# The experts' last 32 slots on 512-wide column tiles with half of the contraction each, in front of the wide products of their stages

## The chip, the cores and the metric

The kernel runs on one core of a Trainium2 chip. The metric is the device time of one execution in microseconds (us); less is better. Engines are called as in the profile: TensorE (PE; its weight loads are PEld), VectorE (DVE), ScalarE (ACT), GpSimd (POOL) and SyncE (SP), which here issues most of the DMAs.

## The reference, cut to what matters

One decoder layer: a mixer of gated linear attention and dilated attention, then a hierarchical mixture of experts, each with a residual, and a final norm. 2048 tokens of 1024 features, 32 experts with 512 hidden features, two experts for a token. The change is in the experts alone:

```python
def expert_block(args):
    toks, e = args
    xb = x[toks]
    hb = jax.nn.silu(xb @ w1[e]) * (xb @ w3[e])
    return hb @ w2[e]
...
y = y.reshape(R, D).astype(jnp.float32) * row_w[:, None]
out = jnp.zeros((M, D), jnp.float32).at[row_tok].add(y)
```

All data are float32. `x` is 2048 x 1024, `w1[e]` and `w3[e]` are 1024 x 512, `w2[e]` is 512 x 1024.

## The kernel before

The part that matters is `moe`. A table in memory holds for each expert 160 slots of a token and its gate. The first 128 slots of an expert are its wide part, the last 32 its narrow part; tokens beyond these go to a loop at the end that is not touched here apart from the call of `up`, `across` and `down`.

Weights. `weights` (L1272) loads the weights of an expert as six tiles `raw` of 128 x 2048 floats, 1 MB each, in the order w1a, w3a, w1b, w3b, w2a, w2b, where a and b are the halves of the contraction. The loads are issued on SyncE's queue; the pool has six buffers. L1288 splits each tile: ScalarE casts it to `hi`, VectorE subtracts and gives `lo`; pool of five buffers each.

Wide part. `turn` (L1310) transposes the 128 gathered tokens (eight transposes on TensorE into `tp`) and splits them into `nh` and `nl`. `up` (L1327) makes 48 products of 128 x 512 for an expert, three for each eighth of the contraction and each of w1 and w3 (L1338 to L1340), in the order w1a, w3a, w1b, w3b, into two PSUM tiles. L1352 and L1353 make `h` of them (silu on ScalarE, product on VectorE). `across` (L1362) transposes `h` (L1365) and splits it into `hh` and `hl` (L1368). `down` (L1378) makes 24 products (L1387 to L1389), scales them by the gate into `y` and adds `y` to the rows of `acc` in memory with an indirect DMA on GpSimd (L1394).

Narrow part. `turn_last` (L1319) transposes the last slots of four experts at once, `R`, into `nr`, which is not split. TensorE multiplies them with the raw float32 weights. A product of only 32 slots fills 32 of 128 columns of the array, so four products stand beside each other in four column groups (`tile_position=(0, 32 * g)`), each with its own 32 partitions of the result `pr`. In `up` the four groups are two halves of 256 columns of w1 and two of w3, each over the full contraction: 8 x 4 matmuls of 256 columns (L1347), behind the 48 wide products in the program. A float32 matmul is two records in the profile, so these are 64. L1358 and L1359 make `hr`, L1373 transposes it, L1375 copies it to `ht`. In `down` the groups are four quarters of w2's 1024 columns: 4 x 4 matmuls of 256 columns (L1402), 32 records, behind the 24 wide products and behind the issue of L1394. L1405 scales the 128 x 256 result into `yr`, and L1406 adds its 128 rows of 1 KB to `acc4`, `acc` seen as quarter rows, at the rows `i4`, which L1203 to L1205 make of the slot table `ir`.

Order. The loop over the experts (L1416) writes for each one: the loads and splits, the gather for the expert after the next, `up`, `across`, `turn` of the next expert, at every fourth expert `turn_last` of the next four, then `down`. This order is only a priority: a scheduler takes, engine by engine and by its own estimate of durations, the first instruction in program order that is ready, and what it finds is the fixed order of that engine's queue. Each engine then works through its queue in order and waits for semaphores where needed. `self.behind` gives single pairs an order. After expert 1, `order` sorts the tokens so that those that are through early can be finished (`finish`: gather of `acc`, norm, scatter to the output) while the last experts run.

Of the kernel before, what the change touches and what calls it, by code (L numbers as in the profile page):

```python
# [56 lines left out]
class Layer:  # L57
# [1113 lines left out]
    def moe(self):  # L1171
        tc, nc, a = self.tc, self.nc, self.a
        with self.moest as st:
# [9 lines left out]
            acc4 = self.acc.rearrange("t (g c) -> (t g) c", g=4)  # L1183
# [3 lines left out]
            i4A = keep.tile([128, NE], I32, name="i4")  # L1187
# [3 lines left out]
            def entries(es):  # L1191
# [10 lines left out]
                f4 = gp.tile([128, NE], F32, name="f4", bufs=1)  # L1202
                nc.vector.tensor_copy(f4[:, es], irA[:, es, 0])  # L1203
                nc.vector.tensor_scalar(f4[:, es], f4[:, es], 4.0, self.gcol, OP.mult, OP.add)
                nc.vector.tensor_copy(i4A[:, es], f4[:, es])  # L1205
# [121 lines left out]
            def up(w, x, nr=None):  # L1327
# [26 lines left out]
                hr = None  # L1354
                if nr is not None:
                    hr = gp.tile([128, 256], F32, name="hr")
                    by, to = (lambda t: t.rearrange("t (p k) -> t k p", k=2)), hr[64:128].rearrange("t (k p) -> t k p", k=2)
                    nc.scalar.activation(to, by(pr[0:64]), AF.Silu)  # L1358
                    nc.vector.tensor_tensor(to, by(pr[64:128]), to, OP.mult)  # L1359
                return h, hr  # L1360

            def across(h, hr):  # L1362
# [3 lines left out]
                hh = gp.tile([128, 4, 128], F32R, name="hh")  # L1366
                hl = gp.tile([128, 4, 128], F32R, name="hl")
                self.crossed = nc.scalar.copy(hh, tp), nc.vector.tensor_tensor(hl, tp, hh.bitcast(F32), OP.subtract)  # L1368
                ht = None
                if hr is not None:  # L1370
                    tr = rps.tile([128, 2, 64], F32, name="r")
                    for c in range(2):
                        nc.tensor.transpose(tr[:, c, :], hr[64:128, c * 128:(c + 1) * 128], self.ident[64:128, 64:128])  # L1373
                    ht = gp.tile([128, 2, 2, 32], F32, name="ht")
                    nc.vector.tensor_copy(ht, tr.rearrange("p c (u s) -> p u c s", u=2))  # L1375
                return hh, hl, ht

            def down(w2, x, it, irs, e=None):  # L1378
                hh, hl, ht = x
# [16 lines left out]
                if ht is not None:  # L1396
                    ir, i4 = irs
                    pr = rps.tile([128, 256], F32, name="r")
                    for k in range(4):
                        raw = w2[k // 2][0]  # L1400
                        for g in range(4):
# [151 lines left out]
```

## Time and profile before

| | us |
|---|---|
| median of 3 runs | 2216.52 |
| lowest, highest | 2212.23, 2219.35 |
| profiled execution | 2223.29 |
| its span | 2221.3 |

Busy times in the span: TensorE 2086.3 us (94%), weight loads 1567.7 (71%), VectorE 1272.1 (57%), ScalarE 1060.2 (48%), GpSimd 474.5 (21%). DMA queues moved 436.59 MB. The experts begin at about 1310 us, with a first expert that waits for its data, and from about 1600 us they run evenly up to 2155 us; after that come the last wide products and the end of the norm.

How to read it: a timeline row has the start and length of an instruction (of several of one kind in a row the count, and the length from the first start to the last end), its engine, line, operation, what it writes and reads, and in brackets how long its engine was idle before it and for whom it waited. The length of a matmul contains its way through the array, so lengths overlap, and what one costs is read from the step to the start of the next. A row of a list of lines gives for all instructions of one line and shape the count, the busy time and the mean length in ns, and behind the second bar the idle time of the engine before them. The clock is the share of 2.4 GHz that TensorE was granted.

### The profile page before, as it was taken

The page shows a single profiled execution, that of the slowest core. Times are in us where ns is not written, and L with a number is a line of the kernel's source. Part 1 is how long each engine was busy: PE and PEld are TensorE (multiplying, and loading weights), DVE is VectorE, ACT ScalarE, POOL GpSimd, SP SyncE. Part 2 cuts the span into 40 slices and gives each one's busy share as a digit, 9 for nine tenths or more (in the row PEclk, how much of TensorE's full clock was granted, in tenths as well). Part 3 has the DMA queues.
Part 4 walks back from the last instruction along what each step waited for, and adds up shares of the span by engine and source line. Part 5 has one row for each costly group of instructions (what it writes and reads, how often), then busy time and mean ns, then how long its engine had stood idle before and what let it go on. Part 6 is the DMA issues. An engine that isn't in the chain of part 4 may idle for free. (4 is left out here: it accounts for less than half of the span.)

```text
span 2221.3 us, 38624 instructions
## 1 busy us (share of the span) xinstructions
PE 2086.3 (94%) x15306; PEld 1567.7 (71%) x15306; DVE 1272.1 (57%) x2452; ACT 1060.2 (48%) x1809; POOL 474.5 (21%) x362
## 2 busy tenths in 40 slices
PE   7999999999997999999999968899999999999990
PEld 7799889799885766666667756567676766767760
DVE  5203336424435466666656766567767677777663
ACT  5412335523323366867723334355555555555552
POOL 2000000000002012351321342523212222222235
PEclk9999999999998999999999969999999999999995
DMA  8333333333316524453368728688888888878886
GB/s 254 109 124 100 114 124 110 102 113 124 109 68 190 178 68 138 146 135 100 88 204 279 238 80 293 198 290 305 298 294 281 307 308 304 305 279 287 307 277 234
DMA packets 189033, 436.59 MB, mean 197 GB/s; under 512 B 35041, under 2 KB 106530, under 8 KB 162978
## 3 DMA queue, kind: packets, MB, share of 16 engines
q1 hardware_dynamic: 139090, 347.65, 44.5%
q0 software_dynamic: 21488, 60.36, 10.4%
q10 hardware_dynamic: 28272, 26.09, 4.0%
q8 instruction: 122, 2.00, 0.4%
q14 instruction: 61, 0.50, 0.1%
HBM read 342.48 MB, written 92.08 MB: 196 GB/s over the span
## 5 line engine op out<-in xcount | busy, mean ns | idle before, releaser
L1288 DVE TENSOR_TENSOR lo<-raw,hi 128x2048 fp32r<-128x2048 f32 x192 | 438.8, 2289 | 121.8 <-ACT hi L1288 121.4
L1288 ACT CAST hi<-raw 128x2048 fp32r<-128x2048 f32 x192 | 365.1, 1906 | 198.5 <-DMA raw<-expert_w 181.0
L564 ACT ACTIVATE P<-P,st 128x256 f32<-128x256 f32 (+1 forms) x384 | 173.9, 455 | 96.8 <-DVE st L562 92.5
L213 PE MATMUL mm<-whi,nh 128*128 128x256 f32 x768 | 219.9, 286 | 0.0
L215 PE MATMUL mm<-whi,nl 128*128 128x256 f32 x768 | 218.1, 284 | 0.0
L214 PE MATMUL mm<-wlo,nh 128*128 128x256 f32 x768 | 217.7, 284 | 0.0
L1340 PE MATMUL mm<-lo,nh 128*128 128x512 f32 x512 | 207.3, 406 | 0.1
L1338 PE MATMUL mm<-hi,nh 128*128 128x512 f32 x512 | 204.6, 400 | 1.1 <-ACT nh L1316 1.1
L1339 PE MATMUL mm<-hi,nl 128*128 128x512 f32 x512 | 201.4, 393 | 0.0
L128 POOL TENSOR_TENSOR ss<-ss,mhalf 128x1 f32<-128x1 f32 (+3 forms) x40 | 34.6, 865 | 699.1 <-DVE ss L127 698.9
L562 DVE CUSTOM_DVE_ANT_0 P<-s,amask 128x256 f32<-128x256 f32 (+1 forms) x384 | 124.9, 362 | 66.2 <-PE s L558 42.6
L190 PE MATMUL mm<-nh,whi 128*128 128x512 f32 x384 | 154.5, 402 | 0.0
L191 PE MATMUL mm<-nl,whi 128*128 128x512 f32 x384 | 153.1, 399 | 0.0
L192 PE MATMUL mm<-nh,wlo 128*128 128x512 f32 x384 | 152.7, 398 | 0.0
L213 PEld LDWEIGHTS mm<-whi,nh 128*128 128x128 f32 x768 | 145.4, 189 | 2.0 <-issue 0.7
L214 PEld LDWEIGHTS mm<-wlo,nh 128*128 128x128 f32 x768 | 145.7, 190 | 0.8 <-DVE wlo L176 0.4
L215 PEld LDWEIGHTS mm<-whi,nl 128*128 128x128 f32 x768 | 144.9, 189 | 0.1
L1347 PE MATMUL r<-raw,nr 128*32 128x256 f32 x2048 | 143.0, 383 | 0.0
L1394 POOL DMA_INDIRECT acc<-y,it x32 | 93.9, 2934 | 228.7 <-ACT y L1391 222.5
L558 PE MATMUL s<-k,q 64*128 64x256 f32 (+1 forms) x768 | 132.8, 416 | 0.3 <-DVE st L562 0.3
L1340 PEld LDWEIGHTS mm<-lo,nh 128*128 128x128 f32 x512 | 96.7, 189 | 43.1 <-issue 19.4
L176 DVE TENSOR_TENSOR wlo<-raw,whi 128x1024 fp32r<-128x1024 f32 x48 | 57.0, 1221 | 112.7 <-ACT whi L175 112.7
(340 smaller groups left out, 4165.0 us busy)
## 6 DMA issues: line engine op xcount, KB each, us to landing
raw<-expert_w SPq DMA_DIRECT2D x192, 1024.0 KB
raw<-w_in ACTq DMA_DIRECT2D x48, 512.0 KB
fb<-fac SPq DMA_DIRECT2D x24, 384.0 KB
x<-x SPq DMA_DIRECT2D x16, 512.0 KB
og<-og SPq DMA_DIRECT2D x32, 256.0 KB
xr<-x SPq DMA_DIRECT2D x32, 256.0 KB
v<-av SPq DMA_DIRECT2D x8, 1024.0 KB
hp<-xr SPq DMA_DIRECT2D x32, 256.0 KB
```

Of the source, the lines that this page charges most:

```text
L190: nc.tensor.matmul(ps, hi[:, k, ms], nh[q][:, k, :], start=k == 0, stop=False)
L191: nc.tensor.matmul(ps, hi[:, k, ms], nl[q][:, k, :], start=False, stop=False)
L192: nc.tensor.matmul(ps, lo[:, k, ms], nh[q][:, k, :], start=False, stop=k == KD - 1)
L213: nc.tensor.matmul(ps[:, j, :], h, hi[:, k, :], start=j == 0 and k == 0, stop=False, skip_group_check=True)
L214: nc.tensor.matmul(ps[:, j, :], h, lo[:, k, :], start=False, stop=False, skip_group_check=True)
L215: nc.tensor.matmul(ps[:, j, :], l, hi[:, k, :], start=False, stop=k == KD - 1, skip_group_check=True)
L564: nc.scalar.activation(P[:, h, 0:w], P[:, h, 0:w], AF.Exp, bias=nm, scale=-1.0, accum_out=dn)
L1288: split = nc.scalar.copy(hi, raw), nc.vector.tensor_tensor(lo, raw, hi.bitcast(F32), OP.subtract)
L1338: nc.tensor.matmul(ps[m], nh[:, k, :], hi[:, kk, :], start=k == 0, stop=False)
L1339: nc.tensor.matmul(ps[m], nl[:, k, :], hi[:, kk, :], start=False, stop=False)
L1340: nc.tensor.matmul(ps[m], nh[:, k, :], lo[:, kk, :], start=False, stop=k == KD - 1)
L1347: nc.tensor.matmul(pr[32 * g:32 * g + 32], nr[:, k, :], raw[:, k % 4, (g % 2) * 256:(g % 2) * 256 + 256], start=k == 0, stop=k == KD - 1, ...
```

## The change

The narrow part gets functions of its own. `up_last` has 16 matmuls of 512 columns instead of 32 of 256: the four column groups are now w1 and w3 with their full 512 columns, each for an even and an odd eighth of the contraction. The two partial sums lie in different partitions of `pr`, so ScalarE copies one pair to `sm`, VectorE adds the other, and then silu and product follow, on 32 partitions of 512 columns. `down_last` has 8 matmuls of 512 columns instead of 16 of 256, with two halves of w2's columns times two eighths of the contraction; the two parts are scaled and added by ScalarE and VectorE, and `yr` has 64 rows of 2 KB, added at the rows `i2` of `acc2` (half rows). `up_last` stands in front of `up` in the program, `down_last`, with the transposes of `hr` and the addition of `yr`, in front of `down`. The tiles `h`, `hh`, `hl`, `hr` and `ht` have one buffer instead of two.

```diff
-                f4 = gp.tile([128, NE], F32, name="f4", bufs=1)
-                nc.vector.tensor_copy(f4[:, es], irA[:, es, 0])
...
+                f2 = gp.tile([64, NE], F32, name="f2", bufs=1)
+                nc.vector.tensor_copy(f2[:, es], irA[0:64, es, 0])
...
+            def up_last(w, nr):
+                pr = rps.tile([128, 512], F32, name="r")
+                for k in range(0, KD, 2):
+                    for g in range(4):
+                        kk, raw = k + g // 2, w[g % 2][k // 4][0]
+                        nc.tensor.matmul(pr[32 * g:32 * g + 32], nr[:, kk, :], raw[:, kk % 4, :],
+                                         start=k == 0, stop=k == KD - 2, skip_group_check=True, tile_position=(0, 32 * g))
+                hr = gp.tile([128, 256], F32, name="hr", bufs=1)
+                sm = gp.tile([64, 512], F32, name="sm", bufs=1)
+                sg = gp.tile([64, 512], F32, name="sg", bufs=1)
+                nc.scalar.copy(sm, pr[64:128])
+                nc.vector.tensor_tensor(sm, pr[0:64], sm, OP.add)
+                nc.scalar.activation(sg[32:64], sm[0:32], AF.Silu)
+                by = lambda t, u: t[:, 256 * u:256 * u + 256].rearrange("t (p k) -> t k p", k=2)
+                for u in range(2):
+                    to = hr[64 + 32 * u:96 + 32 * u].rearrange("t (k p) -> t k p", k=2)
+                    nc.vector.tensor_tensor(to, by(sm[32:64], u), by(sg[32:64], u), OP.mult)
+                return hr
...
-                pr = None
-                if nr is not None:
-                    pr = rps.tile([128, 256], F32, name="r")
-                    for k in range(KD):
-                        for g in range(4):
-                            raw = w[g // 2][k // 4][0]
-                            nc.tensor.matmul(pr[32 * g:32 * g + 32], nr[:, k, :], raw[:, k % 4, (g % 2) * 256:(g % 2) * 256 + 256],
-                                             start=k == 0, stop=k == KD - 1, skip_group_check=True, tile_position=(0, 32 * g))
-                h = gp.tile([128, 512], F32, name="h")
+                h = gp.tile([128, 512], F32, name="h", bufs=1)
...
+            def down_last(w2, hr, ir, i2, e):
+                ht = across_last(hr)
+                pr = rps.tile([128, 512], F32, name="r")
+                for k in range(0, 4, 2):
+                    raw = w2[k // 2][0]
+                    for g in range(4):
+                        kk, f = g // 2, g % 2
+                        nc.tensor.matmul(pr[32 * g:32 * g + 32], ht[:, k // 2, kk, :], raw[:, kk, f * 512:f * 512 + 512],
+                                         start=k == 0, stop=k == 2, skip_group_check=True, tile_position=(0, 32 * g))
+                yr = yp.tile([64, 512], F32, name="yr", bufs=2)
+                nc.scalar.activation(yr, pr[64:128], AF.Copy, scale=ir[64:128, 1:2].bitcast(F32))
+                nc.vector.scalar_tensor_tensor(yr, pr[0:64], ir[0:64, 1:2].bitcast(F32), yr, op0=OP.mult, op1=OP.add)
+                added(nc.gpsimd.indirect_dma_start(out=acc2, out_offset=bass.IndirectOffsetOnAxis(ap=i2, axis=0),
+                                                   in_=yr, in_offset=None, compute_op=OP.add), e)
...
-                h = across(*up((w1, w3), x, nr[:, :, at:at + 32]))
+                hr = up_last((w1, w3), nr[:, :, at:at + 32])
+                h = across(up((w1, w3), x))
...
-                down(w2, h, itA[:, e], (irA[:, e], i4A[:, e:e + 1]), e)
+                down_last(w2, hr, irA[:, e], i2A[:, e:e + 1], e)
+                down(w2, h, itA[:, e], e)
```

`across_last` has the two transposes of `hr` and the copy to `ht` as they were.

## Rows read from the trace of the kernel before

**Rows 1.** Busy time by stretch: from:to us, length, engines' busy us, clock, DMA share, GB/s

```profile
core 0: us, PE busy (x) PEld busy (x) DVE busy (x) ACT busy (x) POOL busy (x), PEclk, DMA share, GB/s
1600.00:2100.00 500.00, 500.00 (x3594) 349.75 (x3593) 356.64 (x259) 287.45 (x218) 120.20 (x63) 1.00 0.85 299
...
2155.00:2222.00 67.00, 9.09 (x68) 5.90 (x62) 20.81 (x26) 16.48 (x29) 41.71 (x37) 0.60 0.67 238
```

**Rows 2.** Timeline of TensorE, one expert: start, length, line, what, count

```profile
1628.56 0.50 PE L1338 MATMUL mm<-hi,nh 128*128 128x512 f32 x1
...
1631.68 0.39 PE L1339 MATMUL mm<-hi,nl 128*128 128x512 f32 x1
1632.00 1.05 PE L1347 MATMUL r<-raw,nr 128*32 128x256 f32 x10
1632.98 0.50 PE L1340 MATMUL mm<-lo,nh 128*128 128x512 f32 x1
1633.32 0.39 PE L1338 MATMUL mm<-hi,nh 128*128 128x512 f32 x1
1633.55 0.39 PE L1339 MATMUL mm<-hi,nl 128*128 128x512 f32 x1
...
1638.65 0.64 PE L1347 MATMUL r<-raw,nr 128*32 128x256 f32 x8
1639.22 0.50 PE L1340 MATMUL mm<-lo,nh 128*128 128x512 f32 x1
...
1641.72 2.79 PE L1347 MATMUL r<-raw,nr 128*32 128x256 f32 x46
1644.44 0.66 PE L1365 MATMUL mm<-ident,h 128*128 128x128 f32 x4
...
1651.93 1.93 PE L1402 MATMUL r<-raw,ht 128*32 128x256 f32 x32
1653.80 0.50 PE L1338 MATMUL mm<-hi,nh 128*128 128x512 f32 x1
```

**Rows 3.** Timeline of TensorE, last narrow piece of the up stage before

```profile
1615.96 3.22 PE L1347 MATMUL r<-raw,nr 128*32 128x256 f32 x54
```

**Rows 4.** Waits of SyncE's queue, 1400 to 2150: total us, times, longest

```profile
SPq L1283 <- PE r L1347: 412.4, 52, 17.4
```

**Rows 5.** Lines of ScalarE and VectorE, 1400 to 2150: busy, mean ns | idle before

```profile
L1358 ACT ACTIVATE hr<-r 64x256 f32<-64x256 f32 x29 | 10.9, 376 | 95.0 <-PE r L1347 84.5 <-remote 10.6
...
L1288 DVE TENSOR_TENSOR lo<-raw,hi 128x2048 fp32r<-128x2048 f32 x172 | 393.4, 2290 | 115.9 <-ACT hi L1288 115.6
...
L1353 DVE TENSOR_TENSOR h<-mm,h 128x512 f32<-128x512 f32 x28 | 19.4, 692 | 53.6 <-PE mm L1340 53.6
...
L1359 DVE TENSOR_TENSOR hr<-r,hr 64x256 f32<-64x256 f32 x29 | 12.4, 427 | 24.1 <-ACT hr L1358 15.3 <-issue 8.6
```

**Rows 6.** Timeline of TensorE, between the stages of the fifth expert

```profile
1464.07 1.09 PE L1313 MATMUL tp<-ident,G 128*128 128x128 f32 x8
...
1465.54 0.34 PE L1373 MATMUL r<-ident,hr 64*128 64x64 f32 x2
1466.30 1.93 PE L1402 MATMUL r<-raw,ht 128*32 128x256 f32 x30 [0.43 <-ACT hh L1368]
```

**Rows 7.** Timeline of TensorE, a narrow down block that is cut

```profile
1600.18 0.63 PE L1402 MATMUL r<-raw,ht 128*32 128x256 f32 x6
...
1601.77 1.91 PE L1402 MATMUL r<-raw,ht 128*32 128x256 f32 x26
```

**Rows 8.** Timeline, first expert: VectorE's cast of the table, TensorE's transposes of `h`

```profile
1340.44 0.18 DVE L1203 CAST f<-ir 128x32 f32<-128x32 int32 x1 [15.44 <-DMA ir<-table]
...
1343.84 1.11 PE L1365 MATMUL mm<-ident,h 128*128 128x128 f32 x4 [6.89 <-DVE h L1353]
```

**Rows 9.** Timeline of GpSimd, tail: last additions to `acc`, first gather behind them

```profile
2173.09 1.61 POOL L1394 DMA_INDIRECT acc<-y,it  x1 [0.31 <-issue]
...
2182.79 1.59 POOL L1406 DMA_INDIRECT acc<-yr,i  x1 [0.30 <-issue]
...
2187.84 2.02 POOL L1235 DMA_INDIRECT raw<-acc,places  x1 [0.19 <-issue]
```

More of the change, by code (lines that the diff above doesn't have):

```diff
@@ L1186, in moe @@
             irA = keep.tile([128, NE, 2], I32, name="ir")
-            i4A = keep.tile([128, NE], I32, name="i4")
+            i2A = keep.tile([64, NE], I32, name="i2")
             irG = keep.tile([128, NE // 4, 2], I32, name="irg")
@@ L1201, in entries @@
                                           reason="the whole table is read")
-                f4 = gp.tile([128, NE], F32, name="f4", bufs=1)
-                nc.vector.tensor_copy(f4[:, es], irA[:, es, 0])
-                nc.vector.tensor_scalar(f4[:, es], f4[:, es], 4.0, self.gcol, OP.mult, OP.add)
-                nc.vector.tensor_copy(i4A[:, es], f4[:, es])
+                f2 = gp.tile([64, NE], F32, name="f2", bufs=1)
+                nc.vector.tensor_copy(f2[:, es], irA[0:64, es, 0])
+                nc.vector.tensor_scalar(f2[:, es], f2[:, es], 2.0, self.gcol[0:64], OP.mult, OP.add)
+                nc.vector.tensor_copy(i2A[:, es], f2[:, es])
             places = keep.tile([128, NT], I32, name="places")
@@ L1325, in turn_last, with up @@
                 return nr
-            def up(w, x, nr=None):
+            def up_last(w, nr):
[16 more added lines that the diff above has]
+                return hr
+            def up(w, x):
                 nh, nl = x
@@ L1353, in up, with across @@
                 nc.vector.tensor_tensor(to(h), by(ps[1]), to(h), OP.mult)
[L1354 to L1362, printed above, removed]
+                return h
+            def across(h):
                 tp = mm.tile([128, 4, 128], F32, name="mm")
@@ L1365, in across @@
                     nc.tensor.transpose(tp[:, k, :], h[:, k * 128:(k + 1) * 128], self.ident)
-                hh = gp.tile([128, 4, 128], F32R, name="hh")
-                hl = gp.tile([128, 4, 128], F32R, name="hl")
+                hh = gp.tile([128, 4, 128], F32R, name="hh", bufs=1)
+                hl = gp.tile([128, 4, 128], F32R, name="hl", bufs=1)
                 self.crossed = nc.scalar.copy(hh, tp), nc.vector.tensor_tensor(hl, tp, hh.bitcast(F32), OP.subtract)
-                ht = None
@@ L1370, in across @@
[L1370 to L1379, printed above, removed]
+                return hh, hl
@@ new lines, in across_last @@
+            def across_last(hr):
+                tr = rps.tile([128, 2, 64], F32, name="r")
+                for c in range(2):
+                    nc.tensor.transpose(tr[:, c, :], hr[64:128, c * 128:(c + 1) * 128], self.ident[64:128, 64:128])
+                ht = gp.tile([128, 2, 2, 32], F32, name="ht", bufs=1)
+                nc.vector.tensor_copy(ht, tr.rearrange("p c (u s) -> p u c s", u=2))
+                return ht
+            def down_last(w2, hr, ir, i2, e):
[12 more added lines that the diff above has]
+                                                   in_=yr, in_offset=None, compute_op=OP.add), e)
@@ L1380, in down @@
+            def down(w2, x, it, e=None):
+                hh, hl = x
                 y = yp.tile([128, D], F32, name="y", bufs=2)
@@ L1395, in down @@
                                                    in_=y, in_offset=None, compute_op=OP.add), e)
[L1396 to L1401, printed above, removed]
-                            nc.tensor.matmul(pr[32 * g:32 * g + 32], ht[:, k // 2, k % 2, :], raw[:, k % 2, g * 256:g * 256 + 256],
-                                             start=k == 0, stop=k == 3, skip_group_check=True, tile_position=(0, 32 * g))
-                    yr = yp.tile([128, 256], F32, name="yr", bufs=2)
-                    nc.vector.tensor_scalar(yr, pr, ir[:, 1:2].bitcast(F32), None, OP.mult)
-                    added(nc.gpsimd.indirect_dma_start(out=acc4, out_offset=bass.IndirectOffsetOnAxis(ap=i4, axis=0),
-                                                       in_=yr, in_offset=None, compute_op=OP.add), e)
             G, R = self.first
@@ L1454, in moe @@
                 x = turn(gx)
-                down(w2, across(*up((w1, w3), x)), it, None)
+                down(w2, across(up((w1, w3), x)), it)
                 m = nc.values_load(cur[:, 2:3], min_val=0, max_val=NT)
```

2 lines of the change are left out of this document (1 added, 1 removed).

## The prediction

> **What bounds the kernel now.** I read the busy time by stage first [rows 1]. From 1600 to 2100 us the core does nothing but experts, and TensorE is busy for 500.00 of 500.00 us at the full granted clock (1.00, the 2.4 GHz level), while VectorE has 356.64, ScalarE 287.45 and the DMA engines a share of 0.85. So this stretch is TensorE's: what an expert costs there is what its matmuls and the joints between them cost. In the tail from 2155 us on TensorE is nearly out of it (9.09 us of 67) and GpSimd, which issues the gathers and scatters, is the busiest. Second, the timeline of TensorE over one expert [rows 2]: from the first wide product of one expert (1628.56) to that of the next (1653.80) are 25.24 us. The narrow products of the last 32 slots do not stand in one block at the end of the up stage, where the program has them. The scheduler has cut them into 10, 8 and 46 matmul records and uses the first two as filling in front of wide products that need a `lo`. Of the 32 up stages 21 end in a piece of 46 and so have this pattern; eight end in a piece of 54 or 52 and have one cut [rows 3]. Third, who the weight loads wait for: 52 times the narrow products of the up stage, 412.4 us in all [rows 4]. A raw tile is free for the next load only when its split and its narrow products are through, and these come last.
>
> **Narrow products, the stream itself.** A block of 32 records takes 1.87 us up to the next instruction, one of 8 takes 0.57 [rows 2]: 24 more cost 1.30, so four records, which are one for each column group, cost 0.217, and a block has 0.57 - 2 x 0.217 = 0.14 of its own. 256 columns in 0.217 us are 0.85 ns a column, two clocks at 2.4 GHz. The four column groups run together and the columns are the price. The change puts 512 columns into each matmul and has half as many: 64 records of an up stage become 32, 32 of a down stage 16, columns unchanged. Doubled, four records cost 0.43, and the up block is 16 x 0.217 + 0.14 = 3.6 us before and after. I cost the wider tile at nothing. The trace has no narrow f32 product of 512 columns; its bounds are the columns alone (a saving of 12 x 0.004 = 0.05 us an expert) and a slower one, which is in the range.
>
> **Joints.** Each cut costs. On the wide side the step into a narrow block is 1632.00 - 1631.68 = 0.32 instead of 0.23 and the first step after it 0.34 instead of 0.23, together 0.20 [rows 2]. On the narrow side three pieces take 0.98 + 0.57 + 2.72 = 4.27 against 3.60 for one block, since 10 and 46 are no multiples of eight and a lone product of one group runs without its three neighbours. Before the transposes a wide product steps on in 0.23 where the narrow block adds 0.09. In front of the wide products, with the four raw tiles landed, the 32 records can go in one block. That the tiles have landed I take from the loads: with the narrow products first, a raw tile of w1 or w3 is free some 15 us earlier than now, a load has most of the 25 us, and a DMA share of 0.85 leaves room. So a three-piece expert saves 0.67 + 2 x 0.20 + 0.09 = 1.16, a two-piece one (0.98 + 3.15 - 3.60) + 0.20 + 0.09 = 0.82; the 3.15 is the 2.72 of 46 records and the 0.43 by which 54 span more [rows 2, 3].
>
> **What the narrow block covered.** Now its 2.7 to 3.15 us lie behind the last wide up product, while ScalarE and VectorE make `h` and before TensorE transposes it. After the change that cover is gone. What remains are the eight transposes of the next expert's tokens, those of `hr`, and the narrow down block. VectorE's product for `h` takes 0.69 [rows 5], the eight transposes span 1.09 [rows 6], so `h` is nearly covered. Then the down block waits for `ht`, which is transposed and copied after it. The fifth expert runs in just this order already [rows 6]: `tp`, `mm`, `hr`, then the narrow down block, with 0.76 from the transpose of `hr` to the block and 0.43 of it idle. I take 0.50 an expert; the ends are nothing (`hr` turned early as filling) and what the third rival below says. Net 0.66 for 21 experts and 0.32 for eight: 13.9 + 2.6 = 16.5 us.
>
> **Smaller terms.** Every fourth expert's transposes of `R` now cut the down block: its two pieces span 0.63 and 1.91 against 1.93 of an uncut one, 0.5 to 0.6 each [rows 2, 7]; where they go beside the next block instead, six of them save 3. Against it, a front block that is cut after all costs about 0.5 (a joint of 0.34 and part of a lone pair); I allow it in six of the 29, 3 us. ScalarE gets a copy of 64x512 out of PSUM, a silu of 32x512 and one half of `yr` for a 64x256 silu of 0.38; at twice the columns and so at most 0.76 each that is at most +1.9 us an expert. VectorE gets an add and half of `yr` at 512 columns (0.69 each) and two products of 256 (0.43 each) for one of these and the old scaling of `yr`, at most +1.8 [rows 5]. ScalarE goes from 57 to at most 67% and VectorE from 71 to at most 81% of an expert's time, hidden beside TensorE unless the order is bad. That `h`, `hh`, `hl`, `hr` and `ht` have one buffer each I cost at nothing: their readers on TensorE stand an expert's down stage ahead of the next writer.
>
> **First expert.** TensorE is idle for 6.89 us until `h`, which stands in VectorE's queue behind the cast of the slot table, which waits 15.44 us for the loads of `ir`, and behind a split [rows 8]. The new cast reads 64 partitions, which the first two of four loads fill. I take 3 us off; ends 0 and 6.9.
>
> **Tail.** Of the last expert the addition of `y` is issued at 2173.09, that of `yr` behind it at 2182.79, and the first gather that needs both at 2187.84 [rows 9]. With the narrow block first, `yr` is added during the wide products and `y` alone is last. The saving lies between the 1.59 us of the issue and 2187.84 - (2173.09 + 5.05) = 9.7 us, with 5.05 the time from the issue of `yr` to that gather; GpSimd has scatters to issue in between, so I take 4. In other experts an addition waits for the one before it on GpSimd; the new order puts the small one some 6 us ahead of the large, and the gathers behind it are two experts early, so nothing.
>
> **Sum.** 16.5 + 3 - 3 + 3 + 4 = 23.5 us. The profiled execution took 2223.29 us (span 2221.3), so by itself 2199.8; the runs' median is 2216.52, 6.8 lower, and 2216.52 - 23.5 = 2193.0.
>
> **Rivals.** (1) The pieces stay. The scheduler orders by readiness, and where w1b and w3b are not thought landed at the start of a stage the narrow block is cut as now. Then only first expert and tail are left: 2216.5 - 7 = 2209.5. For it speaks that the blocks are cut now though the program has them whole; against it, that the loads get free earlier.
> (2) Slower: `ht` or `h` stands behind a split of 2.29 us on VectorE [rows 5], and TensorE, which takes its queue in order, waits in front of the narrow down block with nothing else to run. Each expert that this hits pays up to 2.29. From ten on (23.5 / 2.29) the gain is gone, from 13 the kernel is slower by what can be told; all 29 would give 2193 + 66 = 2259, 18 of them 2234. For it: four new operations on VectorE and less cover. Against it: over the traced stretch VectorE was idle and waiting when `h` became due [rows 5], and the 0.43 of idle time [rows 6] is far below one split. The Trainium skill (TensorEngine Tiling (Array Packing), PSUM Bottleneck) warns that tiling does not speed up the way out of PSUM, which may become the bottleneck, and advises both ScalarE and VectorE for it, as the change does; no row here shows that bottleneck so far.
> (3) The number of instructions is itself a price, so that half of them is a gain. By the rows four records cost their columns and 0.004 us, so this would be below 2 us, and the mechanism has little for it; should the 96 records of an expert each have a price in a part of the trace that the merged rows hide, every 10 ns of it would give 48 x 32 x 0.01 = 15 us, and 2155 would need 25 ns. The Trainium skill (the same page, Instruction Overhead) puts about 60 cycles on each matmul, as an estimate 25 ns at 2.4 GHz, which is that 2155; the 0.217 us for four speak against it.
>
> **Chances.** Forecast 0.62, pieces stay 0.20, slower 0.15, count of instructions 0.03. The forecast itself runs from 2173 (no idle, better tail) to 2212 (idle near 1 us). The range over the cases is 2170 to 2225: above it is most of rival 2, below it rival 3. A measurement of this kernel can tell about 0.3%, 6.6 us: faster than 2209.9 are 0.57 of the forecast, 0.06 of rival 1 and rival 3, 0.66; within it 0.05, 0.13 and 0.02 of rival 2, 0.20; slower 0.14.
>
> **What would show it.** In the profile after: 32 records of the up block together in front of 48 wide products without a cut, and 24.3 to 24.7 us from one expert's up stage to the next; idle before the narrow down block near 0.4 us; casts of raw tiles no longer waiting for loads; the last addition of `y` followed by the gathers. It is wrong if four 512-column records take clearly more than 0.43 us, if the blocks are cut, or if TensorE's idle time in a steady expert is over 1.2 us.

## The result, and the profile after

The changed kernel takes 2233.3 us, the median of six runs (2232.17 to 2242.32), and the kernel before 2215.62 us in six runs on the same chip: ratio 1.008, 95% interval 1.0067 to 1.0093. The forecast was 2193 us in a range of 2170 to 2225. The kernel became slower by 17.7 us where 23.5 were to be gained, and the time lies outside the range. Of all executions told of below, one of `e12` took 5285.14 us and counts in no ratio.

The two profiled executions are only 9.7 us apart (2233.01 against 2223.29, spans 2231.1 and 2221.3), since that of before lies 7.7 over its median. I cut both by the start of the transposes of `h` of an expert, counted from 0, and by TensorE's last instruction:

| stretch | before, us | after, us | after - before |
|---|---|---|---|
| start to the first expert | 1343.84 | 1338.79 | -5.05 |
| first to fourth expert (0 to 3) | 94.35 | 81.98 | -12.37 |
| fourth to 31st expert (3 to 30) | 691.73 | 721.32 | +29.59 |
| 31st expert to TensorE's end | 35.04 | 42.33 | +7.29 |
| TensorE's end to the end | 56.39 | 46.64 | -9.75 |

So the loss is in the steady experts, 29.59 us over 27 of them, 1.10 each, and the ends pay part of it back. The busy time of the steady stretch answers to [rows 1]; columns are from:to, length, and the busy time of each engine with its number of instructions, then the granted clock, the DMA share and GB/s.

```profile
core 0: us, PE busy (x) PEld busy (x) DVE busy (x) ACT busy (x) POOL busy (x), PEclk, DMA share, GB/s
1600.00:2100.00 500.00, 470.90 (x2519) 304.86 (x2518) 356.25 (x283) 297.31 (x243) 118.16 (x60) 0.99 0.84 285
```

TensorE is no longer busy throughout: 29.1 us of 500 are idle. VectorE does as much as before (356.25 against 356.64), though fewer experts go by. Who is waited for, from 1400 to 2150 us of the kernel after (total us, times, longest):

```profile
SPq L1283 <- PE r L1393: 317.9, 56, 14.4
SPq L1283 <- PE r L1334: 263.3, 56, 15.9
...
ACT hi L1288 <- PE mm L1411: 122.0, 27, 7.2
...
PE mm L1372 <- DVE h L1366: 30.5, 23, 2.8
ACT hi L1288 <- PE mm L1360: 28.8, 43, 1.1
...
ACT hi L1288 <- DMA raw<-expert_w: 21.2, 12, 3.3
```

L1372 are the transposes of `h`, L1366 VectorE's product for `h`. TensorE waits in front of nearly every down stage, 23 times in this list. The loads are what the prediction expected of them: the casts of a raw tile wait 12 times for a load; the same row of the kernel before reads:

```profile
ACT hi L1288 <- DMA raw<-expert_w: 173.4, 154, 3.4
```

Instead they wait for the buffer `hi`, which a wide product still reads (L1411 in the down, L1360 in the up stage). What that does to `h` stands in the timeline of all engines at the end of one up stage of the kernel after (start, length, line, what, idle time before it and its releaser):

```profile
1681.24 1.91 ACT L1288 CAST hi<-raw 128x2048 fp32r<-128x2048 f32 x1 [0.20 <-ACT sg L1341]
...
1682.74 0.85 DVE L1345 TENSOR_TENSOR hr<-sm,sg 32x256 f32<-32x256 f32 x2
...
1683.17 0.60 ACT L1365 ACTIVATE h<-mm 128x512 f32<-128x512 f32 x1
...
1683.62 2.29 DVE L1288 TENSOR_TENSOR lo<-raw,hi 128x2048 fp32r<-128x2048 f32 x1
...
1683.95 1.03 PE L1313 MATMUL tp<-ident,G 128*128 128x128 f32 x8
...
1684.92 0.33 PE L1381 MATMUL r<-ident,hr 64*128 64x64 f32 x2
...
1685.84 0.68 DVE L1366 TENSOR_TENSOR h<-mm,h 128x512 f32<-128x512 f32 x1
...
1686.57 0.66 PE L1372 MATMUL mm<-ident,h 128*128 128x128 f32 x4 [1.32 <-DVE h L1366]
```

The cast of the next expert's second tile (w3a) ends at 1683.15. Its split on VectorE (2.29 us) then starts at 1683.62, just before the last wide product and the silu of `h` are through, and the product for `h`, on which TensorE waits, runs behind it. VectorE's rows around `h` in the kernel before are:

```profile
1641.89 0.69 DVE L1353 TENSOR_TENSOR h<-mm,h 128x512 f32<-128x512 f32 x1 [1.80 <-PE mm L1340]
1642.50 2.28 DVE L1288 TENSOR_TENSOR lo<-raw,hi 128x2048 fp32r<-128x2048 f32 x1
...
1650.39 2.29 DVE L1288 TENSOR_TENSOR lo<-raw,hi 128x2048 fp32r<-128x2048 f32 x1 [2.11 <-ACT hi L1288]
...
1653.26 2.28 DVE L1288 TENSOR_TENSOR lo<-raw,hi 128x2048 fp32r<-128x2048 f32 x1
```

The first of these splits is the expert's own (w2b); those at 1650.39 and 1653.26 are the next expert's w1a and w3a. Over 27 experts (from the fifth on) the split of w3a starts 10.9 to 13.9 us behind the product for `h` in the kernel before. In the kernel after it starts 2.21 us in front of it in 20 of them, and in four more the split of w1a does. Ahead of its wait at 1686.57 in the kernel after, TensorE has only the eight transposes of the next tokens and those of `hr`: the narrow up block that lay here before [rows 2] is gone. Between the fourth and the 31st expert TensorE's idle time adds up to 37.07 us (0.94 before).

### The profile page after: what moved, and what is told of

The parts are those of the page before. It is cut to its first block, busy times and chain, and to the rows that moved or that the text cites. A ratio compares the mean times of both kernels' runs of the same rounds, so it can differ in the third digit from the quotient of the medians.

```text
span 2231.1 us, 35747 instructions
## 1 busy us (share of the span) xinstructions
PE 2074.0 (93%) x13770; PEld 1521.1 (68%) x13770; DVE 1305.6 (59%) x2516; ACT 1106.4 (50%) x1873; POOL 495.4 (22%) x362
## 5 line engine op out<-in xcount | busy, mean ns | idle before, releaser
L1360 PE MATMUL mm<-hi,nl 128*128 128x512 f32 x512 | 203.2, 397 | 0.0
L1361 PE MATMUL mm<-lo,nh 128*128 128x512 f32 x512 | 201.0, 393 | 0.0
L1334 PE MATMUL r<-raw,nr 128*32 128x512 f32 x1024 | 144.1, 603 | 0.3 <-DMA raw<-expert_w 0.3
L1359 PEld LDWEIGHTS mm<-hi,nh 128*128 128x128 f32 x512 | 96.8, 189 | 37.8 <-ACT hi L1288 8.4
```

The source lines that it names most:

```text
L1334: nc.tensor.matmul(pr[32 * g:32 * g + 32], nr[:, kk, :], raw[:, kk % 4, :], start=k == 0, stop=k == KD - 2, skip_group_check=True, tile_po ...
L1359: nc.tensor.matmul(ps[m], nh[:, k, :], hi[:, kk, :], start=k == 0, stop=False)
L1360: nc.tensor.matmul(ps[m], nl[:, k, :], hi[:, kk, :], start=False, stop=False)
L1361: nc.tensor.matmul(ps[m], nh[:, k, :], lo[:, kk, :], start=False, stop=k == KD - 1)
```

## Experiments

Each is told with its ratio to the kernel before on the same chip and the 95% interval.

**Place or width?** The change does two things at once, new places and 512-column tiles. `e1_wide_behind` has the tiles in the old places, `e2_narrow_front` the old 256-column tiles in the new places.

```diff
 e1: def up(w, x, nr):  wide products; then
+                pr = last_products(w, nr) if nr is not None else None
                 h = gp.tile([128, 512], F32, name="h", bufs=1)
 ...
-                down_last(w2, hr, irA[:, e], i2A[:, e:e + 1], e)
                 down(w2, h, itA[:, e], e)
+                down_last(w2, ht, irA[:, e], i2A[:, e:e + 1], e)
 e2: up_last and down_last of the changed kernel with
+                pr = rps.tile([128, 256], F32, name="r")
+                for k in range(KD):
```

> The 512-wide tiles alone: the narrow products, the transposes of hr and the addition of yr stand behind the wide products again, as in the kernel before. If the loss of 17 us comes from the place (the narrow up block no longer covers the wait for h), this runs like the kernel before, 2214 to 2220 us, with no idle time in front of the transposes of h. If it comes from the width (dearer cuts, more evacuation on ScalarE and VectorE), it is near the changed kernel, 2228 to 2236 us.

> The place alone: tiles of 256 columns over the full contraction as before, but in front of the wide products of each stage. If the place costs the 17 us, this is near the changed kernel, 2225 to 2236 us, with about 1.3 us of idle time in front of the transposes of h in most experts. If the width costs them, it is near the kernel before or below it, 2208 to 2218 us.

e2: 2243.17 us, ratio 1.0069 (1.0044 to 1.0094), as the changed kernel, with the same wait:

```profile
PE mm L1366 <- DVE h L1360: 28.9, 21, 9.6
```

So the place is enough to lose the time, without the width. It doesn't clear the width: between the fourth and the 31st expert e2 loses 14.8 us (706.51), half of the changed kernel's 29.6, with 31.2 us of idle time against 37.07 and narrow up products of 105.1 us against 116.7. There the wide tile has a price of its own, in blocks that are cut (see the last section). The single buffers of `h`, `hh`, `hl`, `hr` and `ht` are in all kernels with the new functions, and no run varies them alone. e1: 2354.17 us, ratio 1.0578 (1.0549 to 1.0607), which neither side expected. TensorE's waits in e1 from 1400 to 2150 us:

```profile
PE mm L1411 <- ACT hh L1377: 56.1, 25, 5.8
PE mm L1412 <- DVE hl L1377: 34.0, 25, 1.7
```

The wait for `h` is gone with the cover in its place, and another stands one step later, for the cast `hh` and the subtraction `hl` of the transposed `h`. The scheduler also gave other work another place there (the narrow down block starts 15 to 25 us behind the transposes of `h`, in the kernel before mostly 7.5), so e1 is no clean test of the width.

**Is it the split in front of `h`?** `e3_h_ht_first` is the changed kernel with one order on VectorE: the split of the next expert's second tile (w3a) comes behind the product for `h` and the copy `ht`. `e4_h_ht_first_whole` also puts the narrow up block behind the last wide down product, so that it stays whole.

```diff
-                nc.vector.tensor_tensor(to(h), by(ps[1]), to(h), OP.mult)
+                self.made = nc.vector.tensor_tensor(to(h), by(ps[1]), to(h), OP.mult)
 ...
+                self.copied = nc.vector.tensor_copy(ht, tr.rearrange("p c (u s) -> p u c s", u=2))
 ...
+                if e > 1:
+                    hold = {1: [(1, self.made), (1, self.copied)]}
                 w1, w3, w2 = weights(e, hold)
 e4, for each narrow up product p:
+                        self.behind(p, self.lastwide, "in one block")
```

> The changed kernel with one order added on VectorE: from the third expert on the split of the next expert's w3a stands behind the product for h and the copy of ht. If the idle time in front of the transposes of h (0.9 to 2.8 us an expert, 36 us between the sixth and the 31st) is the 2.29 us split in front of h, it goes, and the time falls by 25 to 35 us to 2198 to 2208 us. If it is the missing cover itself, the wait only moves to the next step (ht, hh) and the time stays within 8 us of 2233 us.

> As the kernel with the order on VectorE, and the narrow up products of an expert stand behind the last wide down product of the expert before, so that they are no longer cut into pieces of 16, 12 and 4 records (4.65 us against 3.57 for one block of 32). If the pieces cost what their steps say, this is 0.7 to 1.1 us an expert below the kernel with the order alone, 20 to 30 us, near 2175 to 2185 us. If the pieces were filling for waits of the down stage (hl), the idle time comes back there and the two are within 8 us of each other.

e3: 2221.45 us, ratio 0.9976 (0.9962 to 0.999): one order takes the ratio from 1.008 to 0.9976. The wait before `h` is gone in the steady experts. Every fourth expert, the one that also transposes `R`, now waits one step later; waits of TensorE in e3 from 1400 to 2150, and VectorE in such an expert:

```profile
PE mm L1411 <- DVE hl L1375: 14.3, 7, 2.1
```

```profile
1691.93 4.48 DVE L1288 TENSOR_TENSOR lo<-raw,hi 128x2048 fp32r<-128x2048 f32 x2
...
1696.33 0.68 DVE L1375 TENSOR_TENSOR hl<-mm,hh 128x512 fp32r<-128x512 f32 x1
```

The splits that had to move let others pass, two of them together in front of `hl`. In e4 this came in nearly every expert (42.3 us in 25 times): 2271.07 us, ratio 1.0203 (1.0177 to 1.0229). It tells nothing on whole blocks, only that a wait moves to the next product that nobody holds.

**All waits taken away.** `e5_dve_order` also holds the split of the third tile (w1b) behind `hl`; `e6_dve_order_whole` is e5 with whole blocks, `e7_narrow_dve_order` is e5 with 256-column tiles.

```diff
-                    hold = {1: [(1, self.made), (1, self.copied)]}
+                    hold = {1: [(1, self.made), (1, self.copied)], 2: [(1, self.crossed[1])]}
```

> The kernel with the product for h and the copy of ht first, and besides the split of the next expert's w1b behind the subtraction that gives hl. In the run without this the experts whose down stage holds the transposes of R took 27.3 to 28.8 us against 24.0 to 25.2 for the others, with 2.06 us idle in front of a wide down product that needs hl, behind two splits on VectorE. If the splits in front of hl are the cause, these fall by 2 to 3.3 us, seven of them, and the time by 14 to 20 us, to a ratio of 0.989 to 0.992 of the kernel before. If the wait moves to the next step, the ratio stays near 0.997.

> The same VectorE order with the narrow up products of an expert behind the last wide down product of the expert before, so in one block. If the pieces only cost (4.7 us against 3.6), it is 5 to 20 us below the same order with pieces. If they fill waits of the down stage, it is up to 10 us above it. The 2 percent that the whole blocks lost without the order for hl should be gone in both cases: there the 2.06 us idle stood in front of the wide down products in 24 experts.

> The width once more, with the waits taken away: tiles of 256 columns in front, and the same three orders on VectorE. If the columns are the price and the width is neutral, it is within 8 us of the 512-wide kernel with the same order. If half the instructions are a gain of their own (25 ns each, 1.2 us an expert), it is some 38 us above. If the wide tile costs in the cuts, it is 10 us or more below.

e5: 2186.53 us, ratio 0.9842 (0.9825 to 0.9859), 33 us below the kernel before and more than was expected of it. The same stretch of e5:

```profile
1600.00:2100.00 500.00, 500.00 (x2741) 333.18 (x2740) 386.72 (x309) 321.27 (x267) 123.89 (x64) 1.00 0.87 306
```

TensorE is busy throughout, and 27 experts take 670.89 us against 691.73 before. From the starts of TensorE's instructions (each counted to the start of the next, less idle time), 27 experts:

| us | before | after | e5 | e6 | e7 |
|---|---|---|---|---|---|
| narrow up (pieces) | 115.3 (79) | 116.7 (64) | 111.7 (54) | 102.2 (33) | 109.8 (61) |
| narrow down (pieces) | 54.0 (36) | 52.6 (27) | 47.8 (27) | 50.3 (27) | 49.7 (27) |
| wide up | 312.0 | 299.8 | 299.3 | 302.6 | 301.3 |
| wide down | 157.1 | 158.8 | 157.7 | 160.8 | 161.0 |
| idle | 0.94 | 37.07 | 0.00 | 11.43 | 13.06 |

The gain of e5 is in the wide up products (12.7 us: joints) and in narrow down blocks that nothing cuts (6.2 us); the narrow up block gives only 3.6, since it still goes in two pieces on average. In e6 it goes whole in 21 of 27 experts and costs 9.5 us less, but the time is 2204.76 us, ratio 0.9933 (0.9917 to 0.9948), 18 us above e5 and outside both expectations: pieces that had been filling are now waits and joints elsewhere. One piece of 32 records in e6, and one of the 64-record block with half the columns in e7 (the trace has 58 of its records):

```profile
1666.79 3.64 PE L1334 MATMUL r<-raw,nr 128*32 128x512 f32 x32
```

```profile
1711.87 3.64 PE L1334 MATMUL r<-raw,nr 128*32 128x256 f32 x58
```

Both are followed by the next instruction 3.57 us after their start. e7 takes 2209.37 us (2208.27 to 2224.01), ratio 0.9975 (0.9951 to 1.0), 23 us above e5, where none of its three expectations lies, with 13 us of idle time, most of it for `hh`, which stood behind a cast on ScalarE.

**Do the orders alone do it?** `e9_before_dve_order` puts the three orders into the kernel before, `e10_wide_behind_dve_order` into e1. (The expectation of e9 names the two tiles the other way round, and that of e13 below calls the second tile the third; the diffs hold.)

```diff
 before.py:
+                if e > 1:
+                    hold = {1: [(1, self.made), (1, self.copied)], 2: [(1, self.crossed[1])]}
```

> The kernel before (256-column tiles, old places) with the three orders on VectorE that the fifth experiment has: the split of the next expert's third tile behind the product `h` and the copy `ht`, that of its second tile behind the subtraction `hl`. Theory: the orders only take away a wait which the new place brought, and the kernel before has no such wait, so that nothing moves: 2214 to 2224 us, ratio 0.997 to 1.003. Rival: the 33 us that the fifth experiment lies below the kernel before come from the orders themselves: then 2185 to 2200 us here.

> The first experiment (512-column tiles with half of the contraction each, in the old places behind the wide products) with the same three orders on VectorE. Theory: its 128 us over the kernel before were splits in front of `hl`, of which one kind is now behind it, so that most of the loss goes: 2200 to 2260 us. Rival: in the old place the two further steps of the 512-column tile (the copy `sm` and the addition into it) stand between the narrow block and `hl` on VectorE and are the loss themselves: over 2300 us. If the width is a gain of its own where nothing waits, it comes out below the kernel before, at 2200 to 2212 us.

e9: 2223.58 us, ratio 0.9999 (0.9985 to 1.0013). The orders bring nothing where nothing waits; they only free what the new places bring. e10: 2296.88 us, ratio 1.032 (1.0292 to 1.0347), better than e1 and still far off, between the two expectations. Its waits, 1400 to 2150:

```profile
ACT hi L1288 <- DMA raw<-expert_w: 212.2, 96, 18.2
...
PE mm L1411 <- ACT hh L1377: 20.0, 27, 1.0
PE mm L1374 <- DVE h L1368: 15.5, 4, 11.2
PE mm L1412 <- DVE hl L1377: 9.6, 9, 1.6
```

The loads are late again, as in the kernel before. Between the fourth and the 31st expert e10 takes 73.9 us more than the kernel before: 37.0 are idle time on the way from `h` to `hl`, 21.3 the narrow up products (136.6 us in 80 pieces), and 14.1 the wide down products (171.2). Of these 14.1, 10.5 are in five experts in which TensorE ran at the lower clock for a while after such a wait (granted clock 0.50 from 1591 to 1595). Why `hh` and `hl` come late there, and whether the single buffers have a part in it, stays open.

**Is the width a gain of its own?** `e13_narrow_cast_behind` and `e14_wide_cast_behind` hold the cast for which e7 waited behind `hh` as well, with 256 and 512 columns.

```diff
-                    hold = {1: [(1, self.made), (1, self.copied)], 2: [(1, self.crossed[1])]}
+                    hold = {1: [(0, self.crossed[0]), (1, self.made), (1, self.copied)], 2: [(1, self.crossed[1])]}
```

> The seventh experiment (256-column tiles in front, three orders on VectorE) with one order on ScalarE more: the cast of the next expert's third tile behind the cast `hh`, for which TensorE waited there (10.1 us in 7 times, a cast of 1.90 us in front of it). Theory: its 23 us over the fifth experiment are the 13 us of idle time and the joints around them, and come from the order, not from the width: without them 2185 to 2196 us, ratio 0.985 to 0.989. Rival: 512 columns are the gain (half as many matmuls): it stays at 2203 us or more, ratio 0.993 or more, with TensorE busy throughout.

> The fifth experiment (512-column tiles in front, three orders on VectorE) with the same order on ScalarE, as the partner of the run before it on the same chip. Theory: TensorE waits for nothing in the fifth experiment, so the order brings it nothing: 2180 to 2195 us, ratio 0.982 to 0.988, and the run with 256 columns lies within 6 us of it. Rival: it lies 10 us or more below the run with 256 columns, and then the width is a gain of its own.

e13: 2231.16 us, ratio 1.0016 (0.9994 to 1.0037); e14: 2207.06 us, ratio 0.9913 (0.9891 to 0.9935). Neither theory holds. The order cost both kernels time, e14 some 0.7% against e5 with little idle time (4.3 us; its narrow up products go in 73 pieces and cost 123.9), and it brought e13 a new wait:

```profile
PE mm L1366 <- DVE h L1360: 15.4, 6, 2.9
```

Those are again splits in front of `h`, and one or two of every four experts take 26.2 to 28.9 us. e14 lies 24 us below e13, the number that was to show the width as a gain, but its condition, that TensorE is busy throughout, is not met: e13 has 19.3 us of idle time. The usual experts of e13 take 24.84 us each, those of e14 24.66 to 25.23 and e5's 24.05 to 25.61. So where nothing waits the columns decide nothing that these runs can tell. Between the fourth and the 31st expert e7 takes 18.9 us more than e5 and e13 8.5 more than e14, in experts with waits or more pieces; 11.1 of the 21.3 by which the profiled e13 is longer than e14 lie ahead of the fourth expert, where all kernels vary. Whether a schedule exists in which 256 columns do as well as e5 was not found.

**The ends.** `e8_tail` is the kernel before with the last expert's narrow down block and its addition in front of the wide ones. `e11_last_hl` is e5 with the products of the final normalisation on VectorE held behind the last `hl`, `e12_last_hl_add` e11 with the final scatters behind the last addition in GpSimd's queue.

```diff
 e8: def down(w2, x, it, irs, e=None):
+                if e == NE - 1:
+                    down_last(w2, ht, irs, e)
 e11: def finish(some, made=None, put=None):
+                    if made is not None:
+                        self.behind(v, made, "what the tensor engine waits for comes first")
 e12:
+                    if put is not None:
+                        self.behind(g, put, "the last addition comes first")
```

> The kernel before, with one change: the last expert's narrow down products and the addition of its yr stand in front of its wide down products. If the tail waits for the second addition, as the step from the issue of y to the first gather says (14.75 us), the time falls by 4 to 10 us, a ratio of 0.9955 to 0.998. If GpSimd's scatters bind anyway, it stays within 2 us.

> The fifth experiment with the final normalisation's products on VectorE behind the subtraction `hl` of the last expert, which otherwise waits for them (3.67 us in front of the last `hr`, 0.40 in front of the last `h`, 1.54 in front of the second wide down product). Theory: TensorE ends 4 to 6 us earlier, and the time falls by 3 to 6 us against the fifth experiment: ratio to the kernel before 0.981 to 0.983. Rival: behind TensorE's end GpSimd's queue of scatters sets the end, and the time is that of the fifth experiment: 0.984.

> The experiment before this one, with the final stage's scatters from the second group on behind the last addition to `acc` in GpSimd's queue. In the fifth experiment that addition is issued 9.4 us after its `y` is ready, and the first gather behind it 7.0 us after that. Theory: the last gathers come 6 to 9 us earlier, and the scatters fill the wait for the addition: 4 to 8 us below the experiment before this one, ratio 0.978 to 0.981. Rival: the scatters only move behind the gathers, the queue's sum stays and sets the end: no gain, within 2 us of it.

e8: 2221.14 us, ratio 1.0011 (1.0 to 1.0023). GpSimd in e8, answering to [rows 9]: the small addition, the large one, the first gather.

```profile
2171.98 2.61 POOL L1388 DMA_INDIRECT acc<-yr,i  x1 [0.20 <-issue]
...
2178.08 2.61 POOL L1409 DMA_INDIRECT acc<-y,it  x1 [0.20 <-issue]
...
2186.17 1.21 POOL L1235 DMA_INDIRECT raw<-acc,places  x1 [2.19 <-issue]
```

The gather comes 1.67 us earlier than before when counted from the start, but in this execution the last expert came 4.41 us earlier: counted from its transposes of `h` (2150.77 against 2155.18) the gather comes 2.7 us later. Scatters stand between the two additions and behind them, and GpSimd is idle for 2.19 us in front of the gather. In the medians there is nothing. In the changed kernel the final normalisation even costs: TensorE waits for `hr` of the last expert behind three of its products (VectorE, then TensorE, kernel after).

```profile
2165.74 3.67 DVE L1250 SCALAR_TENSOR_TENSOR G<-G,ss,fg 128x1024 f32<-128x1024 f32 x3 [3.02 <-POOL ss L128]
2169.44 0.88 DVE L1345 TENSOR_TENSOR hr<-sm,sg 32x256 f32<-32x256 f32 x2
...
2170.47 0.31 PE L1381 MATMUL r<-ident,hr 64*128 64x64 f32 x2 [4.22 <-DVE hr L1345]
```

e11 takes this away: its last expert comes 25.02 us after the one before, against 28.54 in e5, and the idle time from there to TensorE's end falls from 5.6 to 0.6 us. From the eleventh expert to the end e11 takes 579.5 us, e12 580.0, e5 585.3. The medians don't show it: ratios 0.9849 (0.9826 to 0.9871) and 0.9846 (0.9819 to 0.9872), so against e5's 0.9842 both stay open within about 5 us. The third and fourth expert of these executions took 6 to 8 us more than in e5; that stretch varies in all kernels (see the smaller terms below). e5 is the best version that a comparison bears out.

## Why the prediction failed, by its own steps

**Stream and width: right for a whole block.** 32 records of 512 columns take 3.57 us up to the next instruction, predicted 3.6; a narrow down block 1.74 to 1.85 against 1.87; and 64 records of half the columns take the same 3.57. The Trainium skill's charge per matmul (TensorEngine Tiling (Array Packing), Instruction Overhead), which the prediction names beside rival 3, would have made the 64 records dearer by 0.8 us, at the 25 ns each that the prediction estimated from it; the trace shows no difference. For a block that is cut, "the wider tile at nothing" was wrong. Over the 3.57 us of a whole block, each further piece of the narrow up block costs some 0.5 us or more at 512 columns (after, e5, e10, e14) and 0.26 to 0.39 at 256 (before, e2, e7, e13; an estimate from the costs and pieces of 27 experts each).

**Joints: right in kind, wrong in number.** The up block was to go whole in front of the wide products. A steady expert of the kernel after has it in pieces of 16, 12 and 4, in the down stage of the expert before, where the scheduler uses it as filling (timeline of TensorE, kernel after):

```profile
1633.96 1.92 PE L1393 MATMUL r<-raw,ht 128*32 128x512 f32 x16
1635.70 1.90 PE L1334 MATMUL r<-raw,nr 128*32 128x512 f32 x16
1638.19 1.91 PE L1334 MATMUL r<-raw,nr 128*32 128x512 f32 x12
...
1645.35 1.05 PE L1334 MATMUL r<-raw,nr 128*32 128x512 f32 x4
```

It has 64 pieces over 27 experts, of which seven have the block whole. So in the kernel after only 6.5 us of the term are left (29.59 us of loss against 36.1 of idle time), some 13 with the fall of the clock that is told below taken out. Still, without waits the joints, with the uncut down blocks, are worth 20.8 us over 27 experts, as e5 shows; before idle time the prediction had 30.9 for 29, which are 28.8 for 27. Against e5 the term was some 8 us too large, and had the right sign and cause. (The count behind it is off by a little: of the 21 stages that end in 46 records one has four pieces, and two of the eight with 54 or 52 have two cuts.)

**What the narrow block covered: this step failed.** I took 0.50 us of idle time an expert ("the third rival" of that sentence is rival 2 of the list); it was 37.07 / 27 = 1.37, and 30.5 of the 37.07 came before the transposes of `h`, not before the narrow down block. The mechanism is rival 2's, a split of 2.29 us on VectorE in front of `h`, to which I gave 0.15; e3 shows it by taking that split away. The reason against it was that VectorE was idle and waiting when `h` became due [rows 5]. That was read from a kernel whose loads were late. In front, the narrow products set the raw tiles free early, which the same prediction said; the casts then wait no longer for loads but for `hi`, and `hi` comes free as the up stage ends, just when `h` is due. The change moved the split into that place by its own success, and the step used the old spacing. That the split moved, by 13 us or more, the rows of VectorE show; that the loads moved it is read from the two lists of waits, and no run separates it from the rest of the new order. Rival 2 was too cheap in one way and too dear in another: it hit nearly all experts, not ten or 18, but with 0.88 to 2.8 us each, since eight transposes cover part of a split. All 29 were priced at 2259 us, and the kernel takes 2233.

**The clock: not in the prediction.** In some experts the wait was long enough for the clock to fall. Busy time of the kernel after in three stretches (the column after POOL is the granted clock):

```profile
1604.00:1608.00 4.00, 1.79 (x7) 0.95 (x7) 4.00 (x5) 2.73 (x4) 1.52 (x1) 0.96 0.99 365
1608.00:1612.00 4.00, 4.00 (x25) 1.03 (x28) 3.67 (x3) 1.69 (x2) 0.00 (x0) 0.61 0.40 98
1612.00:1616.00 4.00, 4.00 (x28) 2.41 (x17) 0.74 (x1) 0.34 (x1) 1.44 (x1) 1.00 0.96 348
```

Ahead of it TensorE had been idle for 2.21, 0.73 and 0.18 us between 1603.1 and 1607.6. The narrow down block at 1608.29 took 3.12 us instead of 1.74. Four of 27 blocks are such (2.54 to 3.34 us); they make up the 4.8 us by which the narrow down products of the kernel after exceed those of e5 in the table.

**Smaller terms.** Loads: right (12 waits instead of 154). `R`: its transposes no longer cut the down block, as predicted. First expert: 5.05 us where 3 were put, within its ends, but one pair of executions doesn't show it: the transposes of `h` start at 1338.8 to 1346.5 us in the ten profiled kernels with this cast and at 1339.8 to 1348.7 in the six with the old one. What the trace shows is that the cast of the table reads 64 partitions and waits less:

```profile
1334.76 0.17 DVE L1203 CAST f<-ir 64x32 f32<-64x32 int32 x1 [9.92 <-DMA ir<-table]
```

Tail: 4 us predicted. TensorE's end to the end became 9.75 us shorter, the last expert 7.29 longer behind the final normalisation; 2.5 are left in the profile, and e8 shows no gain in the time. The 12.37 us in the first experts were not predicted: in the profiled run of before, TensorE waits for `hr` in the third expert, while ScalarE's silu is held up.

```profile
1404.97 0.38 ACT L1358 ACTIVATE hr<-r 64x256 f32<-64x256 f32 x1 [10.57 <-remote]
...
1405.86 0.36 PE L1373 MATMUL r<-ident,hr 64*128 64x64 f32 x1 [5.22 <-issue]
```

The step from the third expert to the fourth takes 39.08 us there and 25.24 in the kernel after, and 25.4 to 37.8 in the experiments, over 30 in some of either place. What ScalarE waits for, the trace doesn't say; it stays open, and it may be why the two profiled runs are closer than the medians.

**The sum again**, between the fourth and the 31st expert: +36.1 us of idle time, and the rest 6.5 us less (29.59 - 36.1), which would be some 6 more without the fall of the clock (the 4.8 above, and 1.5 in two pieces of the next narrow up block). Without waits and clock e5 has -20.8. Against the prediction's 28.8 less for joints and 13.5 more for idle time over 27 experts, the cover is 22.6 us off and the joints, which stayed cut, with the clock 22.3. Of the gain that was predicted a part is there in the kernel after, and most of it once nothing waits (e5); the cover that was taken away cost more than it.

## What to carry to other kernels

Before work is moved away from in front of a wait, list what runs on the other engines in that place after the move, not before it: an edit that sets buffers free early also moves the work that waits for them, and it may land in front of the one product on which the bound engine waits. An idle engine in the old trace is no cover if the edit changes what it was idle for. Then give the list of operations on the short way (here `h`, `ht`, `hh`, `hl`) an order of their own ahead of long work that has slack, all at once: with one of them held, the wait went to the next, and each order given alone to a greedy scheduler rearranged the rest (e4, e13, e14).

## What the runs showed of the hardware

The price of a short wait is not only its length: after 2.21, 0.73 and 0.18 us of idle time in a row, and after single ones of 2.50, 2.80 and 4.08 us, the next narrow down block ran slower (2.54 to 3.34 us), while after single ones of 0.88 to 1.55 us it took its usual 1.74 to 1.85. In the four us after each of these four the granted clock was 0.57 to 0.66 (0.61 in the row above), a mixture of the two levels (1.2 and 2.4 GHz), and 1.00 four us later in that row; in e13, after 2.91 us of idle time, it was 0.50 over the three us in which TensorE ran again. A single one of 2.20 us in the second expert of the kernel after was followed by 1.00 (1370.2 to 1374.2 us).

A whole block of four-column-group products costs by its columns: 32 records of 512 and 64 of 256 both take 3.57 us. A piece of the narrow up block costs by sets of eight records (four products, one for each group), full or not. At 512 columns and the full clock (after, e1, e3, e5, e6, e10, e11 and e14, between the fourth and the 31st expert), pieces of 2, 4, 6 and 8 records took 0.95 to 1.00 us up to the next instruction, of 10 to 16 records 1.82 to 1.85 (1.84 for the 12 above), of 18 to 24 2.67 to 2.78, of 26 to 32 3.55 to 3.63; at 256 columns 10 and 12 records took 0.98 and 0.99. So in e5 a block cut into 16 and 16 cost 3.68 us and one cut into 18 and 14 cost 4.52: a cut between sets costs 0.11 us, and a cut inside one costs about a set, 0.86 us at 512 columns and 0.43 at 256.
